# A decoder layer on one core: up-projection always on both token halves, embedding projection stored ahead, one queue of weights, token blocks of 352

## The chip, the cores and the metric

The kernel runs on 1 core of one Trainium2 chip. The metric is the device time of one execution in microseconds (us), the median of three runs. The engines are TensorE (PE, matmuls), VectorE (DVE), ScalarE (ACT), GpSimd (POOL), and SyncE (SP), which issues most of the DMAs here.

## What is computed

One layer of a decoder for 1024 prompt tokens and 8 x 4 new tokens (1056 columns in all): two token mixers, then a feed-forward network with a convolution, then a per-layer embedding. The change touches what comes after the mixers:

```python
x = x + mixed @ lw['w_out']                       # 1024 x 1024
# conv_ffn
up = rmsnorm(x, lw['g_ffn']) @ lw['w_up']         # 1024 -> 2 * 2816
full = concat([buf, up])                          # two earlier rows
conv = conv_b + sum(full[tap:tap + s] * conv_w[tap] for tap in range(3))
a, v = split(conv, 2)
x = x + (gelu(a) * v) @ lw['w_down']              # 2816 -> 1024
# per-layer embedding
x = x + sigmoid(rmsnorm(x, lw['g_ple']) @ lw['w_ple_gate']) * (p @ lw['w_ple_proj'])   # p: 256 wide
```

## The kernel before

Activations lie with channels on the 128 partitions and tokens along the columns. Every operand is split into a high and a low part of type fp32r (`split`, L81 to L83: ACT casts the high part, another engine subtracts it for the low part), and every product is three matmuls: high x high, high x low, low x high (`mm3`, L85 to L88). A weight tile of 128 x 512 with both parts is called `wx` and has four buffers; it is made of half of a `raw` tile of 512 KB that a DMA brings from DRAM. The weight tiles are made in a fixed order (`wseq`) by `ahead`, up to three ahead of PE. The stages that matter here, with the times of the profiled execution:

- **Merge** (until 1074 us). The last of the mixers; its matmuls are 352 columns wide.
- **w_out** (1074 to 1211 us). Two token halves of 528 columns (`h`), eight output tiles each (`o`), 48 matmuls of 264 columns per tile. Its weights don't come through `raw`: `wload` (L1132) has a single landing buffer `ws` for a whole 128 x 1024 slice; ACT casts it to `wh`, POOL subtracts to `wl`, and only then the next slice may land. The result is added to the residual (`xp`, L1701), stored to DRAM (`dx2`) and squared for the norm. While the second half runs, the operands of the first half for the up-projection are made (`operands`: scale, then sums and splits of 264 columns).
- **Up** (1211 to 1732 us). The up-projection uses a two by two scheme with seven products instead of eight (`ORDER`), on quarters of 264 columns. `up_pair` makes one pair of tiles (gate and value) of the 22 pairs. Since the second half's operands aren't ready yet, pairs 0 to 3 first run on the first half alone, then pairs 4 to 21 run on both halves, and then pairs 0 to 3 on the second half: 26 items (`occ`). Between the products `step` does one piece of the convolution of the pair before (`post`) and one piece of other work (`todo`: in the first four items the operands of the second half). A finished pair is stored to DRAM (`dhid`). A product is 12 matmuls on one half, 24 on both.
- **Down and embedding** (1732 to 2154 us). Three token blocks of 384, 384 and 288 columns (`block`). For each: eight tiles of the down-projection in six weight tiles each, 66 matmuls per tile (`pd`); then per output tile the gate projection (24 matmuls, `pu`) and the embedding's projection (6 matmuls, `proj`), the last elementwise steps (`rest`), a transpose and the store. The sums of the norm are taken after the first gate, its rows are spread after the first `proj`. The hidden activations of the next block are loaded from `dhid` and split during the gates; those of the first block while the last four items of the up-projection run. Weights arrive in `raw` two units ahead of their split; all low parts are subtracted on POOL. The embedding's input is loaded and transposed in each block (`p_turn`).

SP issues its DMAs in order: an issue that waits for a buffer holds up all that stand behind it.

## Time and profile before

| | us |
|---|---|
| median of 3 runs (2148.17 to 2152.28) | 2149.35 |
| the profiled execution, its own time | 2155.55 |
| its span, from the first to the last instruction | 2153.8 |
| PE busy, share of the span | 1987.4 (92%) |
| DVE / ACT / POOL busy | 1217.2 / 933.9 / 1077.4 |
| moved by DMA | 209.18 MB, mean 97 GB/s |

Busy shares are means over stages with different limits. PE's busy time is taken from pipelined matmuls whose ends are modelled, so the spacing of their starts says more than their length. The granted clock is a share of full speed: 1.00 means 2.4 GHz throughout, and a mean below it that a part of the stretch ran at 1.2 GHz. "Idle before, releaser" is the time that an engine stood still ahead of an instruction and what ended it.

### The profile page before, as it was taken

To read this page: it belongs to the slowest core of one execution; us is meant where nothing else is said; L and a number is where in the kernel's file an instruction comes from. 1 tells how busy PE (TensorE), PEld (TensorE's weight loads), DVE (VectorE), ACT (ScalarE), POOL (GpSimd) and SP (SyncE) were. 2 spreads that over 40 slices of the span, in tenths; PEclk is the share of its full clock that TensorE was granted. 3 is DMA by queue.
4 is the path that set the end of the run, shared out by engine and by line. 5 is a ranking of instruction groups with operands and counts; after the bars stand their busy time and mean duration, and the time that the engine had idled before them with its cause. 6 is when DMAs were issued, how large, how long until landed. Compare 5 with 4: busy or idle time off the path is not lost.

```text
span 2153.8 us, 35915 instructions
## 1 busy us (share of the span) xinstructions
PE 1987.4 (92%) x13281; PEld 1862.9 (86%) x13281; DVE 1217.2 (57%) x2386; ACT 933.9 (43%) x1940; POOL 1077.4 (50%) x1119
## 2 busy tenths in 40 slices
PE   7998999989998899999987769999999789999998
PEld 6897888888786688889977759999999689899898
DVE  5517522355878756655516697788787941412322
ACT  5522332344665455443313344444444444534444
POOL 1106331112223222223435687788787866677687
PEclk9999999999999889989998879999999899999999
DMA  7412222153311000033443321222212364653753
GB/s 237 124 21 66 59 71 62 57 149 104 84 51 45 10 12 2 1 133 103 123 151 101 97 74 56 90 63 87 89 61 87 121 190 121 203 172 112 219 167 110
DMA packets 300824, 209.18 MB, mean 97 GB/s; under 512 B 38097, under 2 KB 284036, under 8 KB 300650
## 3 DMA queue, kind: packets, MB, share of 16 engines
q1 hardware_dynamic: 284382, 193.50, 30.2%
q10 hardware_dynamic: 16268, 13.39, 1.9%
q8 instruction: 105, 1.72, 0.3%
q14 instruction: 69, 0.57, 0.1%
HBM read 163.04 MB, written 42.46 MB: 95 GB/s over the span
## 4 chain that ended last, share of the span: by engine, by line
PE 71%; DVE 11%; DMA 6%; POOL 5%; ACT 4%; issue 3%; SPq 1%; ACTq 0%; POOLq 0%; DVEq 0%
PE q L1839 19%; PE pd L86 4%; PE pd L87 4%; PE pd L88 4%; PE pm L87 4%; PE pm L88 4%; PE pm L86 4%; PE pt L86 2%; PE pv L1376 2%; DMA ws<-w_out 2%; PE pt L88 2%; PE pt L87 2%; POOL wl L83 2%; PE p L86 1%; PE p L88 1%
## 5 line engine op out<-in xcount | busy, mean ns | idle before, releaser
L1839 PE MATMUL q<-X,wx 128*128 128x264 f32 x3696 | 479.5, 292 | 39.7 <-ACT wx L1673 14.4
L1839 PEld LDWEIGHTS q<-X,wx 128*128 128x128 f32 x3696 | 470.3, 195 | 48.3 <-ACT wx L1673 19.9
L83 POOL TENSOR_TENSOR wx<-raw,wx 128x512 fp32r<-128x512 f32 (+1 forms) x216 | 258.4, 1207 | 112.7 <-ACT wx L82 111.3
L82 ACT CAST wx<-raw 128x512 fp32r<-128x512 f32 (+1 forms) x216 | 123.3, 572 | 190.6 <-PE pd L88 134.0
L86 PE MATMUL pd<-hd,wx 128*128 128x384 f32 (+1 forms) x528 | 171.4, 325 | 3.1 <-ACT wx L82 3.1
L87 PE MATMUL pd<-hd,wx 128*128 128x384 f32 (+1 forms) x528 | 170.5, 323 | 0.0
L88 PE MATMUL pd<-hd,wx 128*128 128x384 f32 (+1 forms) x528 | 170.4, 323 | 0.0
L1890 DVE SCALAR_TENSOR_TENSOR cv<-up,cw,cv 128x1024 f32<-128x1024 f32 (+2 forms) x104 | 153.0, 1476 | 25.5 <-ACT cv L1881 25.4
L88 PE MATMUL pm<-xh,wl 128*128 128x352 f32 x384 | 126.7, 330 | 0.0
L87 PE MATMUL pm<-xl,wh 128*128 128x352 f32 x384 | 126.2, 329 | 0.0
L86 PE MATMUL pm<-xh,wh 128*128 128x352 f32 x384 | 126.0, 328 | 0.0
L2065 DVE TENSOR_TENSOR xb<-pd,xb 128x384 f32<-128x384 f32 (+1 forms) x24 | 12.6, 524 | 194.8 <-PE pd L88 194.8
L1673 ACT CAST wx<-raw 128x512 fp32r<-128x512 f32 x130 | 80.2, 617 | 93.2 <-PE q L1839 59.2
L1358 POOL TENSOR_TENSOR Pt<-Pt,mstT 128x128 f32<-128x128 f32 x64 | 30.6, 480 | 174.9 <-ACT Pt L1357 174.9
L86 PEld LDWEIGHTS pd<-hd,wx 128*128 128x128 f32 x528 | 99.6, 189 | 3.4 <-ACT hd L82 3.3
L88 PEld LDWEIGHTS pd<-hd,wx 128*128 128x128 f32 x528 | 99.7, 189 | 0.0
L87 PEld LDWEIGHTS pd<-hd,wx 128*128 128x128 f32 x528 | 99.6, 189 | 0.0
L83 POOL TENSOR_TENSOR wl<-ws,wh 128x1024 fp32r<-128x1024 f32 x24 | 58.8, 2450 | 74.7 <-ACT wh L82 63.5
L88 PE MATMUL q<-X,wl 128*128 128x264 f32 x256 | 78.2, 306 | 18.1 <-POOL wl L83 18.1
L83 POOL TENSOR_TENSOR wl<-wst,wh 128x1024 fp32r<-128x1024 f32 x16 | 39.3, 2455 | 102.7 <-ACT wh L82 98.6
L1674 DVE TENSOR_TENSOR wx<-raw,wx 128x512 fp32r<-128x512 f32 x78 | 85.7, 1099 | 7.7 <-ACT wx L1673 7.7
L1674 POOL TENSOR_TENSOR wx<-raw,wx 128x512 fp32r<-128x512 f32 x52 | 71.3, 1372 | 28.4 <-ACT wx L1673 26.4
(694 smaller groups left out, 5704.4 us busy)
## 6 DMA issues: line engine op xcount, KB each, us to landing
raw<-w_up SPq DMA_DIRECT2D x52, 512.0 KB
raw<-w_down SPq DMA_DIRECT2D x48, 512.0 KB
raw<-w_ple_gate SPq DMA_DIRECT2D x24, 512.0 KB
dhid<-cv SPq DMA_DIRECT2D x18, 528.0 KB
raw<-w_down SPq DMA_DIRECT2D x24, 384.0 KB
raw<-dhid SPq DMA_DIRECT2D x22, 384.0 KB
wst<-w_in SPq DMA_DIRECT2D x16, 512.0 KB
cb<-cache_ckv SPq DMA_DIRECT2D x64, 128.0 KB
```

The costliest lines, as they stand in the source:

```text
L82: A.copy(hi, src)
L83: (eng or G).tensor_tensor(lo, src, hi.bitcast(F32), OP.subtract)
L86: PE.matmul(out, lh, rh, start=start, stop=False)
L87: PE.matmul(out, lh, rl, start=False, stop=False)
L88: PE.matmul(out, ll, rh, start=False, stop=stop_)
L1358: G.tensor_tensor(Pt[:, :128], Pt[:, :128], mstT, OP.add)
L1376: PE.matmul(W["pv"][:, j, :DV + 1], Pts[k][:, q0:q0 + 128], Vb[hp][:, k, e], start=k == 0, stop=k == i)
L1673: A.copy(w[:, 0], s)
L1674: (G if m in (2, 5, 4) else V).tensor_tensor(w[:, 1], s, w[:, 0].bitcast(F32), OP.subtract)
L1839: PE.matmul(o_, l_, r_, start=start and k + x == 0, stop=k + x == 5, skip_group_check=not start)
L1890: V.scalar_tensor_tensor(C[:, :L_], U[:, tp:tp + L_], w[tp], C[:, :L_], op0=OP.mult, op1=OP.add)
L2065: V.tensor_tensor(xb[o], pd, xb[o], OP.add)
```

## The change

- `w_out` no longer uses `wload` (but for its first slice): its slices land in the five `raw` tiles and are split by halves into `wx` like all other weights. In the first token half DVE subtracts all low parts; in the second POOL and DVE take turns.
- One list (`rseq`) holds every load into `raw` from `w_out` to the end, the embedding's input and weights and the hidden activations among them; each time a `raw` tile has been used up, `pull` issues the next load of the list.
- The embedding's input is transposed during the second half of `w_out`, and its projection is computed for all tokens in a stage of its own between `w_out` and the up-projection: 16 groups of 12 matmuls of 264 columns. ACT copies the result, SP stores it to DRAM (`dpp`), and the blocks load it back per tile (`pe`). The operands of the second half are made (`B_steps`) in this stage and, for two of the seven products, in the first pair.
- The up-projection then runs all 22 pairs on both halves. The hidden activations of the first block are loaded and split during the last pair, into the memory of the operands that this pair has just used up. The last piece, one channel tile of 128 written by the last pair, follows when that pair has been stored.
- The blocks are 352 columns wide. In the first one, tiles 0 and 1 first take weight tiles 0 to 3 each, then 4 and 5. The low parts of the down and gate weights are subtracted on POOL and DVE in turns. The norm's rows are spread after the third gate has begun; the last addition goes from POOL to DVE.

Where `w_out` begins, SP's issues were:

```order
L1590 DMA ga<-dga 128x1056
L1136 DMA ws<-w_out 128x8x128 x2
L1692 DMA xp<-dxt 128x528 x10
L1136 DMA ws<-w_out 128x8x128
L1702 DMA dx_72<-xp 128x528
L1692 DMA xp<-dxt 128x528 x4
L1136 DMA ws<-w_out 128x8x128
```

and now are:

```order
L1591 DMA ga<-dga 128x1056
L1137 DMA ws<-w_out 128x8x128
L1655 DMA raw<-w_out 128x8x128 x3
L1800 DMA xp<-dxt 128x528 x8
L1655 DMA raw<-w_out 128x8x128 x3
L1811 DMA dx_72<-xp 128x528
L1800 DMA xp<-dxt 128x528 x2
```

Three slices are issued ahead of the residual's tiles and three more behind them, where one at a time was issued.

On DVE, after the norm of the second half is spread (`t`), the scaling of the second half (`xp<-xp,gt,t`) stood between the additions (`up`), the weights (`wx`) and the convolution (`cv`) of the single items:

```order
L1730 COPY t_12373<-pt 128x16
L1862 TENSOR_TENSOR up<-q,up 128x264
L1753 SCALAR_TENSOR_TENSOR xp<-xp,gt,t_12373 128x528 x4
L1674 TENSOR_TENSOR wx<-raw,wx 128x512
L1866 TENSOR_TENSOR up<-q,up 128x264
L1753 SCALAR_TENSOR_TENSOR xp<-xp,gt,t_12373 128x528 x2
L1674 TENSOR_TENSOR wx<-wsum,wx 128x512
```

and now all operands follow one another (`M` are low and high parts; each pair of names is one product's operand):

```order
L1839 COPY t_12374<-pt 128x16
L1860 SCALAR_TENSOR_TENSOR xp<-xp,gt,t_12374 128x528 x4
L1748 TENSOR_TENSOR wx<-wsum,wx 128x512
L1860 SCALAR_TENSOR_TENSOR xp<-xp,gt,t_12374 128x528 x4
L1852 TENSOR_TENSOR M_13769<-xp,M_13768 128x264 x2
L1866 TENSOR_TENSOR xp<-xp 128x264 x2
L1852 TENSOR_TENSOR M_13769<-xp,M_13768 128x264 x2
L1866 TENSOR_TENSOR xp<-xp 128x264 x2
L1875 TENSOR_TENSOR xp<-xp 128x264 x4
L1852 TENSOR_TENSOR M_13819<-xp,M_13818 128x264 x4
L1852 TENSOR_TENSOR M_13874<-xp,M_13873 128x264 x2
```

No addition of the first pair stands between them.

On ACT, where the down-projection begins, the casts of the hidden activations (`hd`) stood between the convolution's steps and needed nothing of the last items:

```order
L82 CAST hd_19165<-raw_19157 128x768
L82 CAST wx_19196<-raw_19108 128x512
L82 CAST hd_19169<-raw_19159 128x768
L1908 ACTIVATE cv_19096<-cv_19096 128x528
L82 CAST wx_19211<-raw_19108 128x256
L82 CAST wx_19228<-raw_19194 128x512
```

and now the last piece (`M10`) stands behind the tenth weight tile of the first block:

```order
L82 CAST wx_19356<-raw_19183 128x512
L82 CAST wx_19371<-raw_19183 128x256
L82 CAST M10_19246<-raw_19244 128x352
L82 CAST wx_19388<-raw_19250 128x512
L82 CAST wx_19403<-raw_19250 128x256
```

It waits for the store of the last pair, and the weight casts behind it wait with it.

The core of the diff:

```diff
+        def pull(n=1):
+            free[0] += n
+            while free[0] and loaded[0] < len(rseq):
+                key, out, src = rseq[loaded[0]]
+                if key[0] == "h" and min(3 * key[2] + 2, NH - 1) not in written:
+                    return
+                loaded[0] += 1
+                free[0] -= 1
+                t = raws[key] = praw.tile([128, T], F32, name="raw", tag="raw", bufs=5)
+                SP.dma_start(out(t), src)
...
+        def wo_unit(h, o, kg):
+            s = k8()(raws["o", h, o])[:, 4 * kg:4 * kg + 4]
+            w = wtile()
+            split(s, w[:, 0], w[:, 1], V if h == 0 or kg else G)
+            if kg:
+                pull()
...
+        def dn_unit(x):
+            kind, o, kg = units[x]
...
+            split(s, w[:, 0, :n], w[:, 1, :n], V if x % 2 else G)
...
-        occ = [(j, 0, 1) for j in range(NJ)] + [(j, 0, 2) for j in range(NJ, NH)] + [(j, 1, 1) for j in range(NJ)]
...
-                    W.append(wload((w_out[:, :, (o + 1) * 128:(o + 2) * 128], 0, 8)))
...
+        A_steps = ([lambda k=k: scale(0, k) for k in range(4)] +
+                   [lambda k=k: (op1(0, k), op3(0, k, G)) for k in range(4)] +
+                   [lambda k=k: (op6(0, k), op2(0, k, G), op7(0, k, G)) for k in range(4)] +
+                   [lambda k=k: (op5(0, k, V), op4(0, k, V)) for k in range(4)])
...
+                if h and 0 < o < 4:
+                    p_turn(o - 1)
                 if h and o > 1:
-                    for _ in range(2):
-                        todo.pop(0)()
+                    for _ in range(3):
+                        if A_steps:
+                            A_steps.pop(0)()
...
+        B_steps = [None, None, lambda: R2.update(r=half_sums()), None, None, None, lambda: half_rows(R2["r"])]
+        B_steps += [lambda k=k: scale(1, k) for k in range(4)]
+        B_steps += [lambda k=k: op1(1, k) for k in range(4)]
+        B_steps += [lambda k=k: (op3(1, k, G), op6(1, k)) for k in range(4)]
+        B_steps += [lambda k=k: op2(1, k, V) for k in range(4)]
+        B_steps += [lambda k=k: op5(1, k, V) for k in range(4)]
...
+            for h in range(2):
+                p_ = acc()
+                for n in range(2):
+                    c = slice(h * HW + n * QW, h * HW + (n + 1) * QW)
+                    for k in range(2):
+                        l_ = [w[:, x, k, (o % 2) * 128:(o % 2) * 128 + 128] for x in range(2)]
+                        mm3(p_[:, n, :QW], l_[0], l_[1], PT["h", k][:, c], PT["l", k][:, c], k == 0, k == 1)
+                e = E[o % 2][:, h]
+                A.copy(e.rearrange("p (n c) -> p n c", n=2), p_[:, :, :QW])
+                SP.dma_start(dpp[o * 128:(o + 1) * 128, h * HW:(h + 1) * HW], e)
+                for _ in range(1 if len(B_steps) > 20 else 2):
...
+        for j in range(NH):
+            up_pair(j, first_pair if j == 0 else last_pair if j == NH - 1 else lambda m: None)
...
-        TB = ((0, 384), (384, 384), (768, 288))
+        TL = ((0, 128), (128, 128), (256, 96))
...
             for o in range(8):
-                pg_ = gate(o)
-                if o == 0:
-                    rst = sums()
-                pp_ = proj(o)
-                if o == 0:
-                    rows(rst)
-                rest(o, pg_, pp_)
+                pgs[o] = gate(o)
+                if b < 2:
+                    hid_split(b + 1, o, V)
+                if o == 0:
+                    rst = sums()
+                    continue
+                if o == 1:
+                    rows(rst)
+                    rest(0, pgs.pop(0))
+                rest(o, pgs.pop(o))
```

## Rows read from the trace of the kernel before

**Rows 1.** The page, part 4: share of the chain that ended last, by engine

```profile
PE 71%; DVE 11%; DMA 6%; POOL 5%; ACT 4%; issue 3%; SPq 1%; ACTq 0%; POOLq 0%; DVEq 0%
```

**Rows 2.** Busy time by stage: from:to, length, engines (instructions), clock, DMA share, GB/s

```profile
core 0: us, PE busy (x) PEld busy (x) DVE busy (x) ACT busy (x) POOL busy (x), PEclk, DMA share, GB/s
1073.90:1211.50 137.60, 110.91 (x792) 106.33 (x791) 53.39 (x76) 36.14 (x64) 71.50 (x48) 0.90 0.41 130
1211.50:1290.30 78.80, 51.66 (x323) 48.37 (x322) 72.64 (x101) 35.32 (x74) 61.89 (x56) 0.78 0.22 67
1290.30:1655.00 364.70, 364.70 (x2962) 362.70 (x2963) 291.91 (x318) 165.92 (x247) 291.90 (x299) 1.00 0.24 76
1655.00:1732.50 77.50, 60.65 (x401) 56.84 (x399) 68.25 (x83) 38.10 (x67) 61.76 (x68) 0.87 0.39 119
1732.50:1876.00 143.50, 135.50 (x781) 133.28 (x781) 45.67 (x68) 67.84 (x122) 96.29 (x83) 0.96 0.56 169
1876.00:2020.00 144.00, 140.93 (x812) 139.36 (x811) 36.79 (x58) 60.90 (x113) 99.63 (x84) 0.99 0.55 161
2020.00:2154.00 134.00, 124.19 (x902) 120.97 (x900) 35.69 (x61) 63.66 (x133) 105.33 (x95) 1.00 0.54 157
```

**Rows 3.** The chain in order of time: start, length, what (the 18 double pairs)

```profile
1290.27 372.54 PE q L1839 x3024
```

**Rows 4.** PE in order of time: matmul starts at 352, 384 and 288 columns

```profile
1067.73 0.32 PE L86 MATMUL p<-yh,wh 128*128 128x352 f32 x1
...
1073.49 0.32 PE L86 MATMUL p<-ath,wh 128*128 128x352 f32 x1
...
1783.11 0.33 PE L86 MATMUL pd<-hd,wx 128*128 128x384 f32 x1
...
1784.67 0.34 PE L86 MATMUL pd<-hd,wx 128*128 128x384 f32 x1
...
2083.93 0.30 PE L86 MATMUL pd<-hd,wx 128*128 128x288 f32 x1
...
2085.12 0.30 PE L86 MATMUL pd<-hd,wx 128*128 128x288 f32 x1
```

**Rows 5.** The chain in order of time, in w_out: one round of the weight slices

```profile
1096.84 4.48 DMA ws<-w_out
1102.55 2.39 POOL wl L83
1104.95 4.78 DMA ws<-w_out
```

**Rows 6.** Busy time while the first half's operands are made (columns as in Rows 2)

```profile
1157.10:1193.60 36.50, 25.35 (x187) 24.21 (x186) 34.43 (x41) 14.98 (x36) 27.35 (x25) 0.91 0.34 102
```

**Rows 7.** DVE, then POOL, in order of time there: one operation alone and beside POOL

```profile
1157.14 8.74 DVE L1753 SCALAR_TENSOR_TENSOR xp<-xp,gt,t 128x528 f32<-128x528 f32 x8
...
1167.10 0.76 DVE L1760 TENSOR_TENSOR xp<-xp 128x264 f32<-128x264 f32 x2
...
1173.43 0.98 DVE L1760 TENSOR_TENSOR xp<-xp 128x264 f32<-128x264 f32 x1
...
1173.18 0.95 POOL L1761 TENSOR_TENSOR xp<-xp 128x264 f32<-128x264 f32 x1
```

**Rows 8.** PE's waits in 1732 to 2154 us: total, times, longest

```profile
PE pt L2145 <- POOL y L2138: 5.6, 5, 2.6
PE pt L2113 <- DVE rst L113: 3.6, 2, 2.0
PE pt L2113 <- DVE msx L2103: 2.3, 1, 2.3
```

**Rows 9.** PE in order of time: three transposes of 128 columns

```profile
1995.02 0.51 PE L2113 MATMUL pt<-ident,rst 128*128 128x128 f32 x3 [1.98 <-DVE rst L113]
```

**Rows 10.** The chain in order of time: a load of hidden activations, first block's gates

```profile
1860.64 6.71 DMA raw<-dhid
```

**Rows 11.** The busiest 50 us of DMA in the blocks (columns as in Rows 2)

```profile
1850.00:1900.00 50.00, 46.53 (x258) 45.43 (x258) 19.03 (x26) 26.56 (x48) 34.84 (x29) 0.94 0.80 239
```

More of the change, by code (lines that the diff above doesn't have):

```diff
@@ new lines, in k8, with cols_ @@
+        def k8(n=8):
+            return lambda t: t[:, :n * 128].rearrange("p (k n) -> p k n", k=n)
+        def cols_(o):
+            return slice(o * 128, (o + 1) * 128)
+        WO = [(h, o) for h in range(2) for o in range(8)][1:]
+        for h, o in WO:
+            raw_load(("o", h, o), k8(), w_out[:, :, cols_(o)])
+            if h == 1 and o < 3:
+                if o < 2:
+                    raw_load(("p", o), lambda t: t[:, :1024].rearrange("p (i d) -> p i d", i=4), ppv[:, 4 * o:4 * o + 4])
+                else:
+                    raw_load(("p", 2), lambda t: t[:32, :256], psv_)
@@ new lines, in body, with wtile, pp_unit @@
+        wsum = {}
+        def wtile(shape=(2, 4, 128)):
+            return wp.tile([128] + list(shape), F32R, name="wx", tag="w", bufs=4)
+        def wo_unit(h, o, kg):
[4 more added lines that the diff above has]
+                pull()
+            return w
+        def pp_unit(u):
+            s = raws["pp", u // 2][:, :1024].rearrange("p (k n) -> p k n", k=2)[:, :, 256 * (u % 2):256 * (u % 2) + 256]
+            w = wtile((2, 2, 256))
+            split(s, w[:, 0], w[:, 1])
+            if u % 2:
+                pull()
+            return w
@@ L1632, in body, with ahead @@
+        wseq += [lambda u=u: pp_unit(u) for u in range(4)]
+        wseq += [lambda j=j, m=m: up_unit(j, m) for j in range(NH) for m in ORDER]
+        wseq += [lambda x=x: dn_unit(x) for x in range(len(units))]
+        wq = []
+        def ahead(n=3):
+            while wseq and len(wq) < n:
+                wq.append(wseq.pop(0)())
         pX = ExitStack()
@@ L1775, in body, with hl @@
-        todo = []
+        XT = [{}, {}]
+        HOME = [{1: "P0", 2: "P2", 3: "P4", 6: "P6", 7: "P8", 5: "P10", 4: "M0"},
+                {1: "M6", 2: "M8", 3: "M10", 6: "M12", 5: "M14", 7: "M2", 4: "M4"}]
+        def hl(h, m, k, src, eng):
+            X = XT[h]
+            if m not in X:
+                f, i = HOME[h][m][0], int(HOME[h][m][1:])
+                X[m] = tuple((ptile if f == "P" else mtile)(i + x) for x in range(2))
+            hi, lo = (x[:, k] for x in X[m])
+            A.copy(hi, src)
+            eng.tensor_tensor(lo, src, hi.bitcast(F32), OP.subtract)
@@ L1792, in body @@
+                if W0:
+                    pull()
+                    ahead()
                 if h and o == 0:
```

608 lines of the change are left out of this document (296 added, 312 removed).

## The prediction

> **What bounds the kernel now.** I read the chain of waits first, then the table by stage, then each stage's waits. PE holds 71% of the chain and DVE, DMA, POOL and ACT share 26% [rows 1], so the end is set by PE nearly everywhere, and what can be won is the time in which PE stands still or runs at the lower clock. The change alters nothing ahead of 1073.9 us, where the same instructions stand in the same order. From there to the end are 1080.1 us [rows 2], and the table shows where PE is full. In the 18 double pairs it never waits: PE busy 364.70 of 364.70 us at clock 1.00. In w_out it is busy 110.91 of 137.60 us at 0.90, in the first four single items 51.66 of 78.80 at 0.78, in the last four 60.65 of 77.50 at 0.87. The blocks are nearly full: 400.6 of 421.5 us. A clock of 0.78 means that part of the stretch ran at 1.2 GHz instead of 2.4, each time behind a stretch in which PE stood still, so a wait costs more than its own length.
>
> What PE would need at full pace comes from the spacing of matmuls: 3024 of 264 columns in 372.54 us, 123.2 ns each [rows 3]; 36 of 352 columns from 1067.73 to 1073.49 us, 160.0 ns; nine of 384 in 1.56 us, 173.3 ns; nine of 288 in 1.19 us, 132.2 ns [rows 4].
>
> **The change, part by part.**
>
> *Weights of w_out.* Before, one slice goes around in 1104.95 - 1096.84 = 8.11 us: it lands in 4.48 us, ACT casts it, POOL subtracts for 2.39 us, and only then the next may land [rows 5]. PE needs 48 x 0.1232 = 5.91 us per tile. That is the stage's wait, and the change removes its cause: three slices are issued ahead of the residual's tiles, into memory that the merge's `yh` gives up 6 us before w_out begins (its last matmuls are those of 1067.73 us [rows 4]), so even the second tile should find its weights. Sixteen tiles are 94.6 us. The transposes of the embedding's input come in here, 18 at 0.51 / 3 us [rows 9], 3 us, and the sums and the spread of the first half's norm stay, some 1 us of PE.
>
> What is late next is DVE in the second half. While it makes the first half's operands it is already full: 34.43 of 36.5 us for 41 instructions, 0.84 us each [rows 6]. One operation of 264 columns takes 0.38 us when POOL is idle, and 0.98 us while POOL works on a like one [rows 7]. Now the same 36 operations stand there, and with them about 7 weight splits, 6 steps of the transposed input and 4 additions of w_out: 53 x 0.84 = 44.5 us, which begin when the norm is spread, 13 us into the half, and so end at 57 us. PE wants the last split at about 48 us. That is a wait of 9 us at the crowded price; at 0.4 to 0.5 us each there is none. As POOL's own share falls (no slices of 1024 columns), I would have taken less, but a wait also lowers the clock: 10 us, bounds 0 and 16. The stage: 94.6 + 4 + 10 = 108.6 us.
>
> *The projection ahead.* 192 matmuls of 264 columns, 23.7 us, with the second half's sums and spread 25.4 us. In the blocks 144 matmuls leave, 48 x (2 x 0.1733 + 0.1322) = 23.0 us, and the 18 transposes, 3 us. By itself this is no gain; it gives PE work while DVE prepares the second half. The copies (ACT), the stores and the later loads (16 and 24 DMAs) lie beside this. SP meets each store behind ACT's copy, and behind it stand weight loads, of which five tiles are already there: nothing is charged.
>
> *The second half's operands.* By the order the spread comes after seven of 16 groups of 12 matmuls, 10.3 us into the stage, and is copied by 12 us. Then DVE has 8 scalings, 34 operations of 264 columns and 2 weight splits. Alone, 34 x 0.38 + 8 x 0.76 + 2 x 0.74 = 20.5 us (a scaling priced as two operations of 264); at 0.84 us each 37 us. They end 32 to 49 us after the stage's start. The first addition of pair 0 stands behind all of them, and the fourth product, which adds to the same accumulator, needs it: that product is due at 25.4 + 3 x 2.96 = 34.3 us. So pair 0 waits between 0 and 15 us. I take 7, the middle: POOL has splits of its own there, but not without a break.
>
> Rows 7 speak for two engines that take turns rather than share. The Trainium skill says so more strictly: in "SBUF — State Buffer", section "Who interferes with whom", VectorE and GpSimd share one pair of ports as an exclusive lock, so an operation with two SBUF inputs waits for the whole GpSimd one; the 0.98 us agree. By it alone both waits would be at their upper ends, which is a rival below.
>
> *22 double pairs.* 168 matmuls x 0.1232 = 20.70 us each, 455.3 us, against 521.0 us for the whole stage before. Nothing in a pair's weights, additions or convolution changes, and with DVE and POOL at 80% PE was never short [rows 2]. What goes is the short item: one product of a single item is 1.48 us of PE, but its weights cost the engines as much as in a double one. The last four items show this without any operands to make: 41.4 us of matmuls took 77.5 us. Into the last pair come seven splits of hidden activations. ACT meets them in order, and two wait for a load that can only be issued when the split before it has freed its tile; such a load was up to 6.71 us late [rows 10]. PE has three weight tiles in hand there: 4 us, bounds 0 and 12. With pair 0: 455.3 + 7 + 4 = 466.3 us.
>
> *Blocks of 352.* 3 x 160.0 = 480.0 ns against 2 x 173.3 + 132.2 = 478.8 ns per weight column block, times 720 matmuls per block: +0.9 us. No gain.
>
> *Waits in the blocks.* 20.9 us of the 421.5 were not PE's. Gone are the three for the norm's rows, 3.6 + 2.3 = 5.9 us [rows 8], since a whole gate now covers them; those for POOL's last addition (5.6 us) become waits for DVE, which I count as the same. New is the last piece of hidden activations: convolution, store, load and split come to 20 us after the last pair's end (8 us of convolution, a late DVE of 4, two transfers of 3 to 7 us). It is needed by the tenth weight tile, after 9 x 12 x 0.16 = 17.3 us, and behind it ACT's casts wait: 6 us. In the gates of two blocks each tile now takes 512 + 528 + 176 + 176 KB, 1.43 MB, in 24 x 0.16 + 0.51 = 4.35 us: 328 GB/s. The busiest 50 us moved 239 GB/s at a share of 0.80, so 299 GB/s at most [rows 11]: 4.77 us per tile, 3.4 us per block, partly covered by five tiles in hand. I take 1 us each; at 239 GB/s it is 13 us each, which is the bound. Idle after: 20.9 - 5.9 + 6 + 2 = 23 us. The stage: 400.6 - 23.0 - 3.0 + 0.9 + 23 = 398.5 us.
>
> Of the loads the Trainium skill would expect less trouble: "HBM Reference", section "Specifications (TRN2)", gives about 358 GB/s per core, which exceeds the 328 wanted. No stretch of 50 us here came near it.
>
> **The sum.** 108.6 + 25.4 + 466.3 + 398.5 = 998.8 us against 1080.1: 81.3 us less. The profiled execution took 2155.55 us of its own time; it becomes 2074.3. The median of the runs lies 6.2 us under that execution, so I predict 2068 us.
>
> **The rivals.**
>
> *Ports all the way.* DVE pays the crowded price throughout: 16 us instead of 10 in w_out, 15 instead of 7 in pair 0, 12 instead of 4 in the last pair: 22 us more, 2090 us. For it speak rows 6; against it that POOL has lost the large slices.
>
> *Room enough.* POOL's gaps let DVE run at nearly the lone price, the splits come in time: 10 + 7 + 4 us less and a little in the blocks, 2045 us. The 18 double pairs speak for it, where both engines are at 80% and PE never waits.
>
> *The loss moves.* The single items lost their time to the second half's operands, and pair 0 inherits the first four items' whole loss of 37 us instead of 7: 2098 us. Against it: the last four lose as much without them.
>
> *One list starves PE, slower than before.* Every load now stands in one line, and one that waits holds up all others. To lose 81 us over the blocks' 111 loads, each must cost 0.73 us; with five tiles in flight the time from a tile's release to its next split must exceed what five cover, 5 x 24 x 0.16 = 19.2 us, by 3.7 us: from 22.9 us on the kernel is slower, about 2155 us. The longest load was 6.71 us [rows 10], with a split some 9. In the gates, where two loads go per tile, five cover only 10.9 us; there it can bite, not for 81 us.
>
> **How the numbers follow.** Forecast 0.48, ports 0.23, room 0.18, moved loss 0.08, starving 0.03. The first three and most of the fourth are within 2036 to 2108 us: below, all waits of operands and splits gone (21 us) and 11 us of the blocks' idle; above, all three at their upper bounds (22 us) and gates short of loads for 18 us. A measurement of this kernel can tell 0.2%, 4 us, from no change. Faster 0.95, same 0.02, slower 0.03.
>
> **What would show it.** w_out within 98 to 115 us, with PE's waits on DVE's splits in its second half and none on DMA; 22 pairs of 20.7 us, waits only in the first and last; DVE's operations of 264 columns near 0.4 or near 0.9 us in the stage ahead of pair 0; the blocks' tiles unchanged per column and no wait for the norm's rows. I am wrong if double pairs wait in the middle of their run, if loads end PE's waits in w_out, or if the gates of the first two blocks take over 45 us.

## The result and the profile after

The kernel after takes **2060.05 us** (median of four runs, 2059.15 to 2061.70), the kernel before 2149.52 us on the same chip: a ratio of 0.9583, with a 95% interval of 0.9566 to 0.9600. That is 89.5 us less; 81.3 were forecast. The profiled execution took 2059.21 us, its span is 2057.2 us and its mean granted clock 0.970. Two of the seven executions of experiment e9 below ran at a lower clock (0.55 and 0.74, 3098.85 and 2671.36 us): its ratio leaves them out, its median of 2069.45 us would be 2068.92 without them, and since its kept trace is one of them, that of e11 is read in its place.

The chain that ended last has moved to PE, and DMA's and POOL's shares have fallen (page of after, part 4, to be held against [rows 1]):

```profile
PE 78%; DVE 11%; ACT 3%; DMA 3%; issue 2%; POOL 2%; SPq 1%; ACTq 0%; DVEq 0%; POOLq 0%
```

The same by stage, with the columns of [rows 2]: w_out, the embedding's projection, pair 0, twenty pairs, the last pair, and the three blocks.

```profile
1071.40:1175.30 103.90, 100.66 (x801) 99.50 (x800) 63.49 (x101) 41.77 (x84) 43.77 (x37) 0.97 0.57 178
1175.30:1203.60 28.30, 26.25 (x212) 25.52 (x210) 18.65 (x35) 14.70 (x32) 15.42 (x17) 1.00 0.52 181
1203.60:1230.50 26.90, 21.94 (x169) 21.84 (x169) 19.24 (x39) 13.14 (x28) 20.51 (x18) 0.94 0.22 70
1230.50:1644.00 413.50, 413.50 (x3362) 410.16 (x3361) 335.05 (x361) 189.76 (x281) 333.03 (x341) 1.00 0.25 78
1644.00:1668.50 24.50, 22.50 (x170) 22.11 (x169) 19.51 (x18) 13.81 (x19) 18.61 (x14) 0.93 0.47 152
1668.50:1798.00 129.50, 122.56 (x750) 119.14 (x748) 73.22 (x100) 66.06 (x118) 51.45 (x41) 0.96 0.69 199
1798.00:1926.00 128.00, 125.31 (x777) 123.50 (x776) 61.60 (x99) 61.04 (x116) 52.34 (x39) 0.99 0.67 196
1926.00:2057.30 131.30, 124.00 (x782) 122.61 (x780) 49.95 (x92) 54.04 (x111) 48.21 (x38) 0.99 0.47 136
```

How to read it: where PE's busy time equals the stretch there is nothing left to win but the work itself. That holds for 413.5 of the 985.9 us. w_out has gone from 110.91 busy of 137.60 at clock 0.90 to 100.66 of 103.90 at 0.97; the eight single items, 156.3 us in [rows 2], no longer exist; the blocks' PE busy time has fallen from 400.6 to 371.9 us. The stages together take 985.9 us against 1080.1, 94.2 less. The merge ahead of them, which is the same in both programs, ended 2.5 us earlier in this execution than in the one of before, and adds that to the difference of the spans.

What is left of PE's waits of a microsecond and more, ahead of the blocks and at their start (PE in order of time: start, length, what, and in brackets the idle time before it and what ended it):

```profile
1159.94 0.51 PE L1941 MATMUL q<-M,wx 128*128 128x264 f32 x2 [1.90 <-ACT wx L82]
1161.62 1.69 PE L1941 MATMUL q<-M,wx 128*128 128x264 f32 x6 [1.17 <-POOL wx L83]
1178.09 0.39 PE L88 MATMUL q<-M,wx 128*128 128x264 f32 x1 [2.05 <-POOL wx L83]
1208.66 3.01 PE L2015 MATMUL q<-P,wx 128*128 128x264 f32 x12 [4.96 <-ACT pe L1983]
1661.06 1.25 PE L2015 MATMUL q<-M,wx 128*128 128x264 f32 x8 [1.90 <-DVE up L2035]
1672.60 1.02 PE L2128 MATMUL pt<-ident,LU 128*18 128x128 f32 x4 [3.05 <-ACT lo__19576 L2130]
```

No load ends one of them itself. In the last pair loads stand in the chain all the same: ACT waits there for two loads of hidden activations, as forecast, 0.64 us shortly before PE's 1.90 and, behind it, longer ahead of this cast:

```profile
1663.19 1.07 ACT L82 CAST M<-raw 128x1056 fp32r<-128x1056 f32 x1 [4.94 <-DMA raw<-dhid]
```

In the blocks PE waited as follows from 1668.5 us on (total, times, longest; the four largest kinds), which answers to [rows 8]. The three waits for the norm's rows are not there. Those for `y`, the output ahead of its transpose, were 5.6 us on POOL and another 2.1 on DVE before (1.3 and 0.8, not among [rows 8]) and are 5.6 us on DVE now. Those for the squares (`sqb`) and the gates' operands (`gg`) are new, 4.0 us together with 0.6 for `gg` on ACT, which is not among these lines:

```profile
PE pt L2233 <- DVE y L2226: 5.6, 6, 2.1
PE pt L2128 <- ACT lo__19576 L2130: 3.1, 1, 3.1
PE pt L2197 <- DVE sqb L2168: 2.0, 2, 1.0
PE pu L87 <- DVE gg L2162: 1.4, 2, 0.7
```

### The profile page after: what moved, and what is told of

It reads as the page before. It is cut to its first block, busy times and chain, and to the rows that moved or that the text cites. A ratio compares the mean times of both kernels' runs of the same rounds, so it can differ in the third digit from the quotient of the medians.

```text
span 2057.2 us, 35869 instructions
## 1 busy us (share of the span) xinstructions
PE 1954.4 (95%) x13329; PEld 1837.9 (89%) x13329; DVE 1253.5 (61%) x2465; ACT 921.1 (45%) x1910; POOL 871.9 (42%) x928
## 4 chain that ended last, share of the span: by engine, by line
PE 78%; DVE 11%; ACT 3%; DMA 3%; issue 2%; POOL 2%; SPq 1%; ACTq 0%; DVEq 0%; POOLq 0%
PE q L2015 21%; PE pm L87 4%; PE pm L88 4%; PE pd L88 4%; PE pd L87 4%; PE pd L86 4%; PE pm L86 4%; PE q L1941 3%; PE pt L86 2%; PE pv L1377 2%; PE pt L88 2%; PE pt L87 2%; PE p L86 2%; PE p L88 2%; PE p L87 2%
## 5 line engine op out<-in xcount | busy, mean ns | idle before, releaser
L2015 PE MATMUL q<-M,wx 128*128 128x264 f32 x2112 | 280.8, 286 | 1.9 <-DVE up L2035 1.9
L2015 PEld LDWEIGHTS q<-M,wx 128*128 128x128 f32 x2112 | 268.5, 189 | 2.1 <-issue 2.1
L83 POOL TENSOR_TENSOR wx<-raw,wx 128x512 fp32r<-128x512 f32 x108 | 146.9, 1361 | 221.5 <-ACT wx L82 212.6
L2015 PE MATMUL q<-P,wx 128*128 128x264 f32 x1584 | 217.3, 286 | 5.1 <-ACT pe L1983 5.0
L82 ACT CAST wx<-raw 128x512 fp32r<-128x512 f32 x226 | 133.3, 597 | 194.2 <-PE pd L88 113.5
L2015 PEld LDWEIGHTS q<-P,wx 128*128 128x128 f32 x1584 | 201.5, 189 | 8.8 <-ACT pe L1983 5.2
L83 DVE TENSOR_TENSOR wx<-raw,wx 128x512 fp32r<-128x512 f32 (+1 forms) x118 | 91.9, 780 | 138.9 <-ACT wx L82 131.9
L86 PE MATMUL pd<-M,wx 128*128 128x352 f32 x528 | 171.4, 325 | 0.0
L87 PE MATMUL pd<-M,wx 128*128 128x352 f32 x528 | 171.0, 324 | 0.0
L88 PE MATMUL pd<-M,wx 128*128 128x352 f32 x528 | 170.9, 324 | 0.0
L2058 DVE SCALAR_TENSOR_TENSOR cv<-up,cw,cv 128x1024 f32<-128x1024 f32 x88 | 143.2, 1627 | 28.3 <-ACT cv L2050 28.3
L1747 ACT CAST wx<-raw 128x512 fp32r<-128x512 f32 x110 | 68.0, 618 | 72.0 <-PE q L2015 47.2
L88 PEld LDWEIGHTS pd<-M,wx 128*128 128x128 f32 x528 | 99.6, 189 | 0.3 <-DVE wx L83 0.2
L86 PEld LDWEIGHTS pd<-M,wx 128*128 128x128 f32 x528 | 99.7, 189 | 0.1
L87 PEld LDWEIGHTS pd<-M,wx 128*128 128x128 f32 x528 | 99.6, 189 | 0.0
L1941 PE MATMUL q<-M,wx 128*128 128x264 f32 x720 | 92.3, 290 | 3.2 <-ACT wx L82 1.9
L1941 PEld LDWEIGHTS q<-M,wx 128*128 128x128 f32 x720 | 90.6, 193 | 4.0 <-ACT wx L82 2.1
```

The lines of the kernel that those rows point to most:

```text
L82: A.copy(hi, src)
L83: (eng or G).tensor_tensor(lo, src, hi.bitcast(F32), OP.subtract)
L86: PE.matmul(out, lh, rh, start=start, stop=False)
L87: PE.matmul(out, lh, rl, start=False, stop=False)
L88: PE.matmul(out, ll, rh, start=False, stop=stop_)
L1747: A.copy(w[:, 0], s)
```

## The experiments

Executions of one kernel differ here by more than the 0.2% of the prediction: the five of e12, which is the kernel after again, lie between 2058.17 and 2063.52 us, the four of e4 between 2050.98 and 2060.71. So the small effects (e5 to e8, e10) are read from traces as well as from times. For the start of the stage they are compared by one distance: from w_out's first matmul to ACT's first copy of pair 1, which takes in w_out, the projection and pair 0. It is 1233.76 - 1071.42 = 162.3 us in the profiled execution of after, and 1237.06 - 1072.03 = 165.0 us in that of e12, which is the same kernel: a distance within 2.7 us of either of the two tells nothing.

**e1: what a single item costs.** The kernel before with two more single items on each side.

```
-        NJ = 4
+        NJ = 6
```

> The kernel before, with NJ = 6 for 4: two double pairs become four single items (six with the first token half, six with the second), nothing else. Theory (a single item costs ACT, DVE and POOL the whole making of its weights, 77.5 us / 4 = 19.4 us in the last four, and PE waits for that): four more singles for two doubles of 20.3 us, 4 x 19.4 - 2 x 20.3 = 37 us more, 2187 us (2178 to 2196). Rival (the first four items wait for the second half's operands, the last four for hidden activations that are read in beside them; a single item with nothing beside it runs at PE's pace, 84 x 0.1232 = 10.35 us): 4 x 10.35 - 2 x 20.3, no more than 1 us, 2150 us, or up to 10 us less since the operands get two more items of room.

Measured: 2171.6 us, a ratio of 1.0098 to before (1.0079 to 1.0117), about 21 us more: neither 37 nor 1. The trace tells why. The kernel now has two single items, the fifth and the sixth, that have neither operands nor hidden activations beside them (e1, busy time by stage, columns as in [rows 2]: these two items, then 16 double pairs; below, PE in order of time, from one place in the fourth item to the same place in the fifth):

```profile
1291.80:1321.00 29.20, 22.98 (x172) 21.87 (x171) 25.19 (x29) 14.47 (x25) 25.71 (x23) 0.96 0.31 91
1321.00:1651.00 330.00, 329.66 (x2683) 326.53 (x2682) 263.17 (x286) 149.20 (x223) 260.96 (x268) 1.00 0.25 77
```

```profile
1289.22 7.72 PE L1839 MATMUL q<-X,wx 128*128 128x264 f32 x60 [2.46 <-DVE up L1862]
1303.19 7.72 PE L1839 MATMUL q<-X,wx 128*128 128x264 f32 x60 [2.01 <-DVE up L1862]
```

The first row spans a little more than the two items (172 matmuls, of which 168 are theirs). From one row of PE to the next such a bare item takes 13.97 us, while PE needs 10.35: it costs 3.6 us more than its matmuls, not 9. DVE and POOL are busy for 12.6 and 12.9 us per item of the row. That the 3.6 us are the weights is not shown: PE's waits there end on DVE's additions, which stand in DVE's queue behind steps of the convolution as well as behind weights. Four bare items for two double pairs of 20.6 us (330.0 / 16) are 15 us more, most of the 21 measured.

What the eight single items lost before has to be counted by the items' own borders, which are not those of [rows 2]. Of the first four items' 336 matmuls 312 stand between 1210.7 and 1290.27 us, so the chain of [rows 3] begins 24 matmuls ahead of the double pairs: they run from 1293.2 to 1665.8 us. The last matmuls of the up-projection are these:

```profile
1729.15 6.86 PE L1839 MATMUL q<-X,wx 128*128 128x264 f32 x39 [0.36 <-DVE up L1856]
```

They end at 1736.0 us. So the first four items took 82.5 us and the last four 70.2, not 77.5, and lost 41 and 29 us, 70 together. That has three sources: 8 x 3.6 = 29 us what a bare item costs beyond its matmuls, 82.5 - 4 x 13.97 = 27 us the second half's norm and operands in the first four, and 70.2 - 55.9 = 14 us what stands beside the last four alone: the hidden activations and the convolution of the new tokens, which this count does not tell apart.

**e2 and e3: what w_out's time hung on.** e2 is the kernel after with w_out's weights as before; e3 keeps the pieces of 512 columns and their engines and takes only the landing tiles away.

```
# e2
-                W0 = W.pop(0) if W else None
+                W0 = W.pop(0)
+                if (h, o) < (1, 7):
+                    W.append(wload((w_out[:, :, cols_((o + 1) % 8)], 0, 8)))
+                else:
+                    ahead()
...
# e3
-            raw_load(("o", h, o), k8(), w_out[:, :, cols_(o)])
...
+                t = raws["o", h, o] = wp.tile([128, 1024], F32, name="ws", tag="ws", bufs=1)
+                SP.dma_start(k8()(t), w_out[:, :, cols_(o)])
```

> The kernel after, with the w_out slices loaded as in the kernel before: one landing tile, one cast and one subtraction on POOL of 1024 columns, a slice per tile of PE. Theory (the round trip of 8.11 us set this stage): the stage grows from 103.9 us to the 137.6 of before, +34 us, 2094 us (2086 to 2100). Rival (the stage lost its time to DVE's and POOL's operand work, which stands there in both kernels): at most 10 us more, up to 2070 us.

> The kernel after, with the w_out slices still split in two pieces of 512 columns on DVE or POOL, but landing in one tile instead of five. Theory (landing in turn is the cause, not the size of the pieces): a round is 4.48 us of landing, some 0.6 of cast, 0.75 to 1.5 of the last subtraction and half a cast and subtraction ahead of it, 6.4 to 7.6 us against 5.91 of PE: 15 slices give 8 to 25 us more, 2068 to 2085 us. Rival (the 1024 columns on POOL were the cause, 2.39 us per slice and an engine of DVE blocked by them): 0 to 4 us more, 2060 to 2064 us.

Measured: e2 2094.46 us (ratio 0.9738, 0.9720 to 0.9756), 34 us above the kernel after; e3 2075.93 us (0.9653, 0.9630 to 0.9675), 16 above it. The stage in the two traces (busy time, e2 and then e3) and, below it, one round after the other in e3's chain in order of time:

```profile
1079.60:1219.90 140.30, 114.93 (x804) 110.86 (x803) 54.27 (x79) 38.54 (x68) 70.75 (x47) 0.88 0.41 132
```

```profile
1072.70:1194.60 121.90, 109.28 (x802) 104.99 (x802) 64.09 (x101) 40.70 (x84) 44.45 (x39) 0.93 0.47 152
```

```profile
1086.56 4.49 DMA ws<-w_out
1093.12 4.19 DMA ws<-w_out
1099.39 4.71 DMA ws<-w_out
```

So the single landing tile is a cause by itself, as the prediction had it, and the gain splits in two. With small pieces a round is some 6.4 us between these rows (6.85 on the mean of the eight from 1086.56 to 1141.37 us), more than PE's 5.91, and the stage 18 us longer than the 103.9 of after; the slice of 1024 columns, which POOL holds for 2.39 us, lengthens the round to the 8.11 us of [rows 5] and costs the other 18. Neither rival has its number. The large slice was half of the matter, though, and whether it would cost anything with five landing tiles was not tried.

**e4: the projection as cover.**

```
-                        mm3(p_[:, n, :QW], l_[0], l_[1], PT["h", k][:, c], PT["l", k][:, c], k == 0, k == 1)
+                        PE.matmul(p_[:, n, :QW], l_[0], PT["h", k][:, c], start=k == 0, stop=k == 1)
```

> The kernel after, with one of the three products of the embedding's projection: 64 matmuls in place of 192; the two correction products are left out. Theory (the projection is cover: DVE's preparation of the second half sets when the pairs can start, whatever PE does): PE has 128 x 0.1232 = 15.8 us less to do and waits about that much longer ahead of and in pair 0, 2058 to 2064 us. Rival (DVE's preparation is nearly done in time, the 5 us of wait at pair 0 are ACT's order alone): 15.8 us less, 2044 to 2047 us.

Measured: 2056.85 us (0.9560, 0.9533 to 0.9586), 3 to 4 us below the kernel after and 1 below the theory's range, where PE has 15.8 us less to do; the distance to pair 1 is 160.3 us against 162.3 and 165.0. What became of the time shows in the projection and pair 0 (e4, columns as in [rows 2]):

```profile
1175.80:1229.00 53.20, 41.91 (x252) 37.96 (x251) 37.67 (x73) 26.81 (x61) 33.72 (x33) 0.81 0.38 130
```

PE stands still for 11.3 us, against 7.0 in these two stages of after; the longest wait, 3.8 us, is for the sums of the squares, the others are short and many, in pair 0 mostly for operands (1.7 us on DVE, 1.5 on ACT) and weights (1.4 on POOL). And its 252 matmuls take 41.9 us, where 252 x 0.1232 = 31.0 would do: the granted clock is 0.81, where the projection and pair 0 of after have 1.00 and 0.94. So PE's lower clock hides more of the 15.8 us than its waits do. The rival falls: most of the projection costs nothing where it stands. That the making of the second half's operands alone sets this, and not the clock as well, is argued from the waits in pair 0 and not shown.

**e5: the two engines and their ports.**

```
-            G.tensor_tensor(b12, b22, b12, OP.subtract)
+            e3.tensor_tensor(b12, b22, b12, OP.subtract)
...
-        B_steps += [lambda k=k: (op3(1, k, G), op6(1, k)) for k in range(4)]
+        B_steps += [lambda k=k: (op3(1, k, V), op6(1, k)) for k in range(4)]
```

> The kernel after, with the eight POOL operations of the second half's operands (op3's splits and its four subtractions) on DVE. DVE then has 52 instead of 44 instructions in the stretch from the spread of the norm to the last operand, POOL only pieces of weights. Theory (the two engines take turns, so a POOL operation with two inputs costs DVE about its own length: DVE's four L1866 took 1099 ns and eight L1860 950 ns beside POOL, where 264 columns take 420 alone): without them DVE saves more than the eight operations add, 4 x 0.7 + 8 x 0.2 + 4 x 0.27 + 22 x 0.05 = 6.6 against 8 x 0.42 = 3.4 us; the preparation ends some 3 us sooner, pair 0 waits 2 us instead of 5, 2056 to 2058 us. Rival (DVE's durations are its own, POOL's operations lie beside them): 8 x 0.58 = 4.6 us longer, pair 0 waits about 9 us, 2063 to 2065 us.

Measured: 2063.16 us (0.9595, 0.9576 to 0.9614), and a distance of 166.6 us. That is the rival's number, but e12, the kernel after again, has 2061.24 and 165.0, so it is only shown that nothing was gained. And DVE's durations are not its own, as the rival said they were. In e5 four subtractions (L1866) and eight scalings (L1860), now without POOL beside them, take 427 and 765 ns against 1099 and 950 in the kernel after; and four others (L1881) that took 420 ns now take 962, because POOL's pieces of pair 0's weights, no longer queued behind operands, run then. DVE's groups in 1191.1 to 1221.7 us of e5 (busy, mean ns of one), POOL's longest operation there, and DVE beside its second half, both in order of time:

```profile
L1860 DVE SCALAR_TENSOR_TENSOR xp<-xp,gt,t 128x528 f32<-128x528 f32 x8 | 5.6, 765 | 0.0
L1881 DVE TENSOR_TENSOR xp<-xp 128x264 f32<-128x264 f32 x4 | 3.8, 962 | 0.0
...
L1866 DVE TENSOR_TENSOR xp<-xp 128x264 f32<-128x264 f32 x4 | 1.5, 427 | 0.0
```

```profile
1200.12 3.89 POOL L1748 TENSOR_TENSOR wx<-raw,wx 128x512 fp32r<-128x512 f32 x1 [15.60 <-ACT wx L1747]
```

```profile
1202.09 0.43 DVE L1871 TENSOR_TENSOR xp<-xp 128x264 f32<-128x264 f32 x1
1202.43 1.87 DVE L1852 TENSOR_TENSOR M<-xp,M 128x264 fp32r<-128x264 f32 x2
1204.22 1.51 DVE L1875 TENSOR_TENSOR xp<-xp 128x264 f32<-128x264 f32 x1
```

The same groups of the kernel after, in 1190.1 to 1215.8 us:

```profile
L1852 DVE TENSOR_TENSOR M<-xp,M 128x264 fp32r<-128x264 f32 x22 | 9.2, 472 | 0.0
L1860 DVE SCALAR_TENSOR_TENSOR xp<-xp,gt,t 128x528 f32<-128x528 f32 x8 | 7.1, 950 | 0.0
L1866 DVE TENSOR_TENSOR xp<-xp 128x264 f32<-128x264 f32 x4 | 4.2, 1099 | 0.0
L1875 DVE TENSOR_TENSOR xp<-xp 128x264 f32<-128x264 f32 x4 | 2.5, 692 | 0.0
L1881 DVE TENSOR_TENSOR xp<-xp 128x264 f32<-128x264 f32 x4 | 1.5, 420 | 0.0
```

The slow operations stand beside POOL operations, and POOL's own 3.89 us, for a subtraction that takes 1.29 us 11 us later, cover a stretch in which DVE first ran at its full pace: the two take turns. But to move POOL's operands to DVE frees nothing while POOL has weights to make in their stead. My expectation counted the savings and forgot what POOL would do next. The wait that the prediction had named now appears: pair 0's fourth product waits for the first addition, which stands behind the whole preparation (e5, PE):

```profile
1222.46 1.91 PE L2015 MATMUL q<-P,wx 128*128 128x264 f32 x7 [7.22 <-DVE up L2027]
```

**e6: the wait at the start of block 0.**

```
...
-                for _ in range(3):
-                    if side:
-                        side.pop(0)()
+                with tc.issue_after(lastmm[0].ins):
+                    for _ in range(3):
+                        if side:
+                            side.pop(0)()
```

> The kernel after, with the transposes of the last rows held behind the third tile of block 0 instead of ahead of its first matmul. They cost 3.05 us of wait and some 1.3 us of the lower clock there. Theory (this wait hides another: the last hidden piece is split at 1689.8 us and used at about 1692.4): PE comes 4.4 us sooner and waits 1 to 3.5 us at that piece or at the weights cast behind it, net gain 1 to 3 us, 2057 to 2059 us. Rival (the last piece came early, the prediction's 6 us for it were simply too many): the whole 4.4 us are gained, 2055 to 2056 us, and no new wait stands in block 0.

Measured: 2061.6 us (0.9596, 0.9578 to 0.9614): nothing gained. Something was hidden behind that wait, but not the last hidden piece, which PE still does not wait for. The down projection starts 4 us earlier against the end of the last pair, and then waits for its weights instead, three times (e6, PE, the two longest; behind them the two ACT rows that explain it):

```profile
1680.91 0.43 PE L86 MATMUL pd<-M,wx 128*128 128x352 f32 x1 [1.15 <-ACT wx L82]
1683.37 0.43 PE L88 MATMUL pd<-M,wx 128*128 128x352 f32 x1 [1.87 <-DVE wx L83]
```

```profile
1679.26 1.08 ACT L2077 ACTIVATE cv<-cv 128x1056 f32<-128x1056 f32 x1 [3.07 <-DVE cv L2061]
1680.25 2.16 ACT L82 CAST wx<-raw 128x512 fp32r<-128x512 f32 x4
```

ACT keeps its order: the last pair's gelu waits 3.07 us for DVE's convolution, and four casts of weights stand behind it.

**e7, e8 and e10: the wait ahead of pair 0.** In the kernel after, ACT's rows there are these; the last line is the copy that pair 0 waited for:

```profile
1203.83 0.41 ACT L1851 CAST M<-xp 128x264 fp32r<-128x264 f32 x1 [2.31 <-DVE xp L1866]
1206.13 0.41 ACT L1851 CAST M<-xp 128x264 fp32r<-128x264 f32 x1 [1.89 <-DVE xp L1875]
...
1208.02 1.09 ACT L1983 COPY pe<-q 128x528 f32<-128x528 f32 x2
```

PE could not start pair 0 because the projection's last accumulators were not copied out, and they were not because ACT's copy stands behind casts of operands that DVE had not made. e7 takes the projection's splits off POOL; e8 also moves the norm's spread and the operands ahead; e10 also makes one step of the operands per group instead of two and holds the steps that remain, the last casts among them, behind the last copy.

```
# e7
-            split(s, w[:, 0], w[:, 1])
+            split(s, w[:, 0], w[:, 1], V)
...
# e8, beside that
-        B_steps = [None, None, lambda: R2.update(r=half_sums()), None, None, None, lambda: half_rows(R2["r"])]
+        B_steps = [None, lambda: R2.update(r=half_sums()), None, None, lambda: half_rows(R2["r"])]
...
# e10, beside both
-                for _ in range(1 if len(B_steps) > 20 else 2):
+                for _ in range(1 if o < 6 or h == 0 else 1):
...
-        while B_steps:
-            B_steps.pop(0)()
+        with tc.issue_after(cp.ins):
+            while B_steps:
+                B_steps.pop(0)()
```

> The kernel after, with the four splits of the projection's weights on DVE, which is idle there, instead of POOL, which is behind with sums for pair 0's weights and with w_out's squares. Theory: the 2.05 us wait at 1178 us goes, and the spread of the norm, which stands at a fixed place of PE's order, comes 2 us sooner, as do DVE's preparation and pair 0: 2 us less, 2058 us. Rival (the squares on POOL set the spread, or DVE's end does not move): 0, 2060 us.

> As e7, and the sums and the spread of the second half's norm stand one and two groups of 12 matmuls earlier, and so do the operands behind them. Theory (DVE's preparation sets pair 0, and its start is the spread): it starts 2 + 3 = 5 us sooner, the 5 us of wait ahead of pair 0 fall to 0 to 2, 2054 to 2057 us. Rival (ACT's order is the cause: the projection's copies stand behind casts that wait for DVE, wherever these start): the wait stays at 4 to 5 us, 2058 us.

> As e8, and the casts of the last operands stand behind ACT's last copy of the projection. Theory (in e8 ACT's copies still wait 2.08 us behind casts that wait for DVE, and that is what is left): no wait ahead of pair 0 or in it, 4 to 6 us less than the kernel after, 2054 to 2056 us. Rival (DVE's preparation is the limit, and casts that come later only delay it): the wait moves into pair 0, behind the first addition, and 2 us are left of the gain, 2058 us.

Measured: 2057.95, 2056.73 and 2058.11 us (0.9575, 0.9564 and 0.9571, each with 0.0016 to 0.0027 either way), with distances of 160.4, 160.6 and 162.0 us. None can be told from the kernel after (0.9583) with certainty, and e8 and e10 not from e7, which each contains. e7 does remove the 2.05 us at 1178 us, and keeps 4.99 ahead of pair 0. In e8 the wait ahead of pair 0 is gone, and e10 lowers what came in its stead; but each time the waits stand elsewhere (e8, then e10, PE):

```profile
1179.90 1.18 PE L1822 MATMUL pt<-ones,t 128*128 128x1 f32 x10 [1.58 <-DVE t L1817]
...
1203.29 0.39 PE L86 MATMUL q<-M,wx 128*128 128x264 f32 x1 [2.08 <-ACT pe L1983]
```

```profile
1200.76 0.39 PE L86 MATMUL q<-M,wx 128*128 128x264 f32 x1 [0.75 <-ACT pe L1983]
1215.69 3.37 PE L2016 MATMUL q<-P,wx 128*128 128x264 f32 x15 [2.54 <-POOL wx L1748]
```

With the spread earlier the sums wait for the last addition of squares; with the copies ahead, pair 0 waits for POOL's weights. Added up from the end of w_out through pair 0, PE's waits are 7.0 us in the kernel after, 5.0 in e7, 4.6 in e8 and 4.9 in e10. So ACT's order set the place of the 4.96 us and not the most of it. That it is the work of DVE and POOL from the end of w_out to pair 0 which does not fit is the reading left, and e10's rival comes nearest to it; no run here makes that work less.

**e9, e11, e12: the short waits of the blocks.**

```
...
-                pgs[o] = gate(o)
+                if o == 0:
+                    gate(0, (0,))
+                    gate(1, (0,))
+                    gate(0, (1,))
+                if o:
+                    gate(o, (1,) if o == 1 else range(2))
...
-                if o == 0:
-                    rst = sums()
-                    continue
...
-                out_turn(o - 1)
+                with tc.issue_after(lastmm[0].ins):
+                    if o == 0:
+                        rst = sums()
+                        continue
...
+                    if o > 1:
+                        out_turn(o - 2)
+            out_turn(6)
```

> The kernel after; in each block the first halves of gates 0 and 1 stand ahead of their second halves, the norm's sums behind gate 0, and each output transposition one gate later. Theory (the short waits of the blocks are each a matter of order: 0.47 + 0.70 + 0.72 us for the last gg, 1.02 + 1.03 for the squares, 0.85 + 0.84 + 0.75 + 0.91 for y, 7.3 us in all): they go and nothing takes their place, 6 to 7.5 us less, 2053 to 2054 us. Rival (what is late is the chain itself: the later spread keeps the three gate accumulators, and gate 3 waits for the first to come free): 0 to 2 us less, 2058 to 2060 us.

> e9 and e10 together, in places that don't meet. If both theories hold, 10 to 13 us less than the kernel after, 2047 to 2050 us; if both rivals hold, 2056 to 2058 us.

> The kernel after as it is, beside e9 to e11 on the same chip, so that differences of 0.2% can be told: 2060 us (2058 to 2063).

Measured: e12, the kernel after again, 2061.24 us (0.9586, 0.9564 to 0.9609); e9 2069.45 us (0.9630, 0.9607 to 0.9652); e11 2073.45 us (0.9649, 0.9627 to 0.9671). e9 is 8 us slower, worse than either theory. e11's trace, whose blocks are e9's, shows what (of e11 itself neither theory nor rival came true): the waits for gg are gone, and the norm's rows are waited for again, twice at length (PE's waits from 1668 us on):

```profile
PE pt L2212 <- DVE rst L115: 5.5, 2, 4.2
PE pt L2212 <- DVE msx L2203: 4.3, 1, 4.3
```

The sums came later, the rows did not, and DVE's chain between them fell in the open. These are the waits of [rows 8] that the change had removed. Without being meant to, e9 undoes that part of the change, and shows that a whole gate between sums and rows is what hid them.

## Why the prediction was right

The forecast of 2068 us was 8 us high, inside its range, and the likeliest case is the one that came. Some of the closeness is luck. The stages together came to 985.9 us, 12.9 under their sum, and the profiled execution to 2059.21, 15.1 under the forecast for it; 7 of these are gone in the medians, since the profiled execution of before lay 6.2 us above its median and that of after 0.8 below. So a few us between the two traces are no effect of the change. By its own steps:

*w_out: 108.6 forecast, 103.9 measured.* The landing tile was a cause and the large slice on POOL the other (e2, e3). DVE was nearly as crowded as forecast: from the spread of the first half's norm on, 54 instructions in 39.33 us busy of 39.40, 0.73 us each against 0.84, and never idle:

```profile
1131.70:1171.10 39.40, 39.33 (x54) 0.91 0.39 122
```

The step that was too dear is what this costs PE: 10 us were charged for weight splits behind it. The splits stand among the operands, not behind them all, and half of the second half's are POOL's. Only 5.3 us came, and not where they were forecast: PE waited 0.2 us for DVE's splits, 1.17 for one of POOL's, and 1.90 for a weight cast on ACT that stood behind the cast of an operand, which had itself waited 3.49 us for POOL (ACT at 1158.95 us); the rest is matmuls at the lower clock.

*Projection: 25.4 forecast, 28.3 measured.* Of the 2.9 us more, 2.05 are the wait for POOL's split of the projection's own weights, for which the forecast had no term.

*Pair 0: 7 us forecast, 6.2 measured, 4.96 of them wait, by another way.* The prediction let DVE's preparation end 32 to 49 us into the stage and took the first addition behind it as the wait. It ended at about 40 us (1215.8 us), in the middle. But the wait fell earlier, on the copy of the projection on ACT, which the prediction had counted as lying beside; by the time of the addition PE had already lost what it would have lost there. e5 brings back the wait that was named. The place was set by ACT's order; that DVE and POOL set the amount is argued (e7 to e10). The sign that was asked for, DVE's operations of 264 columns near 0.4 or near 0.9 us, came out between: the 34 of the kernel after took 0.57 us on the mean (e5's last rows).

*The 22 pairs: 466.3 us forecast, 464.9 measured.* The sum holds. The twenty pairs in the middle took 20.68 us each without a wait, and the last pair 24.5, 3.8 more than the 20.70 of full pace, where 4 were forecast: 1.90 us of wait, with the first of the late loads in its chain, and matmuls at the lower clock. But the reason given for the gain does not hold. The prediction charged the loss of a single item to its own weights, since "the last four items show this without any operands to make: 41.4 us of matmuls took 77.5 us". The row of 77.5 us begins 11 us ahead of these items and has 401 matmuls where they have 336; they took 70.2 us. They had hidden activations to read in, and e1 shows that a bare single item costs 14.0 us. So less than half of the 70 us lost were what a short item costs by itself. The 27 us of norm and operands are paid for mostly under the projection (e4), the rest is pair 0's wait; the 14 us in the last four have shrunk to the 3.8 us of the last pair. Why the same activations cost so much less in one double pair than in four single items was not tried; that DVE and POOL were busy for 68.25 and 61.76 us of the row of 77.5 [rows 2] is only an argument. So the rival in which the loss moves was nearer to the truth in its mechanism than its 0.08 says, and what was held against it, that the last four lose as much, is not so (29 us against 41): it fell because the projection covers it.

*Blocks: 398.5 us forecast, 388.8 measured.* PE's work was put 3.6 us too high (375.5 against 371.9 busy): the row of the first block begins at 1732.5 us, 3.5 ahead of the up-projection's last matmuls, so these were counted as the block's. The idle time was put 6 too high (23 against 16.9). It is 20.9 less the 5.9 of the rows, as forecast, less 2.1 on `y`, and 4.0 more for the new waits on `sqb` and `gg`, of which the forecast had none. The 6 us for the last hidden piece are the step that failed. It came when forecast, some 20 us behind the last pair (ACT):

```profile
1688.74 0.49 ACT L82 CAST M<-raw 128x352 fp32r<-128x352 f32 x1 [1.90 <-DMA raw<-dhid]
```

PE wanted it later, though: the last rows' transposes stood ahead of the down projection, 3.05 us of wait and then some ten matmuls at the slower spacing. e6 shows that without them weights are waited for there. The start of block 0 costs about 4.5 us whichever of these comes last, and before it was no cheaper (PE waited 3.08 us at 1739.09 us for a weight cast); the forecast had added a further cause to that without asking which ends last. The norm's rows went as forecast (e9 shows by what), and blocks of 352 cost nothing that a row shows.

*Loads.* 2 us were charged to the gates of two blocks, and no wait for a load was measured. These gates took some 32 us each, where 45 would have been a sign of being wrong, and their DMA engines were among the busiest of the stage:

```profile
1894.00:1926.00 32.00, 29.47 (x177) 28.25 (x178) 26.55 (x47) 17.93 (x37) 9.22 (x7) 0.95 0.88 257
```

257 GB/s at a share of 0.88 is 292 GB/s when full, the 299 of [rows 11] again; that what did not fit had been loaded ahead is the likely reason, and not shown. The Trainium skill's 358 GB/s ("HBM Reference", section "Specifications (TRN2)") was not reached here either, and was not needed.

*The ports.* For 264 columns 420 ns without POOL and 1099 beside it agree with the Trainium skill's exclusive lock ("SBUF — State Buffer", section "Who interferes with whom"). The rival built on it, 2090 us, fell because the crowded price was not paid throughout (0.57 us on the mean ahead of pair 0, 0.73 in w_out, against the 0.84 it went by), and where it was paid PE had the projection to do (e4).

## What to carry over

Before a loss is charged to one cause, look for a stretch where that cause stands alone, or make one: items charged with 9 us each cost 3.6 alone, and one number changed showed it. Before a row is read as the time of some work, count its instructions: 401 matmuls in the row of four items that have 336 told that its borders were not theirs. Work that is moved into a gap in which another engine prepares something was nearly free here, and its removal worth nearly nothing. Where a wait is taken away and the time stays, ask for the next one in the same engine's queue (a cast behind a gelu, a copy behind a cast): several waits that start from one place cost about their longest here, not their sum.

## What was not expected of the hardware

One DVE operation on 264 columns took from 0.42 us to over 1.5, and one POOL subtraction of 512 columns from 1.29 to 3.89 us, according to what the other engine ran. POOL can wait through a whole run of DVE's operations: in the kernel after two of its splits of 264 columns, 0.77 us each 11 us earlier, took 7.05 us together from 1210.12 us on, while DVE went on at 0.36 us per operation. So a duration read in one stage is no price for another. After the 3.05 us of idle PE's matmuls of 352 columns started 0.29 us apart instead of 0.16 for some 2.5 us, and the time of two executions of the same kernel differed by 2.7 us over the same 165 us: pair 0 of e12 had clock 0.88 where that of after had 0.94, with the same wait of 4.96 us ahead of it.
